# One token block's expert weights are added up in DRAM by indirect scatters

## The chip, the cores and the metric

The kernel runs on one core of one Trainium2 chip. The metric is the device time of one execution in microseconds; the time before is 1711.16 us, the median of three runs (1708.38 to 1712.05). Engine names are those of the profile: PE (TensorE), DVE (VectorE), ACT (ScalarE), POOL (GpSimd), SP (SyncE).

## The reference

One decoder block over 512 tokens of width 1024: two mixers with gates, then a product-key expert layer (PEER) over 16384 experts, then a norm. The change touches the expert layer alone:

```python
q = (xb @ w_q).reshape(TB, H, 2, PEER_HALF)             # 8 heads, two halves
s = jnp.einsum('thpc,phnc->thpn', q, sub_keys)           # 128 scores per half
s1, i1 = lax.top_k(s[:, :, 0], K); s2, i2 = lax.top_k(s[:, :, 1], K)      # K = 16
cand = (s1[..., :, None] + s2[..., None, :]).reshape(TB, H, K * K)
top_s, pos = lax.top_k(cand, K)                          # 16 experts per head
eidx = take(i1 * 128 + i2, pos)                          # 128 experts per token
g = softmax(top_s)
h = jnp.einsum('tkd,td->tk', u[eidx], xb)
out = jnp.einsum('tk,tkd->td', gelu(h) * g, v[eidx])
```

## The kernel before

The 512 tokens are four blocks (0 to 3) of 128. The kernel does the mixers first (projections, HGRN2 chains, gates, attention, up and output projections, to about 465 us). Then come three stages of the expert layer.

**Picks** (about 465 to 691 us). For each head h, `query` makes the two halves' queries for all four blocks, `scores` their scores, and `picks` (L670) finds with DVE's maximum and index instructions the 16 experts per token: e12 holds i1 and i2. Block 0's experts are written to eidx (L709), those of blocks 1 to 3 to iw12 (L711, ACT). Between the heads stand u chunks (`u_chunk`, L739): chunk j multiplies the 128 experts i*128+j with all tokens of blocks 1 to 3 (24 matmuls of 384 columns), Gelu on ACT, result to h_d in DRAM. Every chunk's weights are loaded by SP's queue and split into a high part (w_hi, ACT, L108) and a low part (w_lo, DVE, L110), double-buffered. 28 of the 128 chunks are done here (UH). After the last head `weigh` (L713) makes the softmax of all heads and blocks: gw0 for block 0, iw12's third plane for the others.

**One-hot stage** (about 692 to 949 us). Another 48 u chunks, and with each one group of 8 tokens of the weight matrix G[i, j, t] = sum of the weights with which token t picked expert i*128+j. `g_block` (L817) transposes a block's i1, i2 and weights; `g_group` (L834) builds one-hot rows on DVE (oz, ow, L845 and L847) and multiplies them on PE (16 matmuls of 128 columns, L855); ACT copies them out (L858), and each 32 tokens go to g_d by SP's queue (2 MB, L873). `work` (L861) lists 3 blocks x 16 groups = 48.

**V stage** (about 949 us to the end). The last 52 u chunks, and for each chunk j the product of G and Gelu(h) on DVE (`v_parts`, L903), split into aH and aL, times the experts' v rows: 18 matmuls of 512 columns, accumulated in PSUM over all 128 chunks. G comes back for four j at once (L901), Gelu(h) from h_d.

**Block 0** goes another way: POOL gathers for each of the 128 picks the 128 u rows (one per token) by an indirect DMA (`row`, L755, 512 KB), DVE multiplies with x (`u_row`, L762); later the same with v rows (`v_row`, L772). Four row buffers. In the picks no row is asked for (R0 = 0), in the one-hot stage one per chunk (R1 = 1, none for the last 8 chunks), in the V stage 2.9 and then 0.95.

The order of an engine's instructions is not the program's: a planning pass orders them by when their inputs are ready in its model of time, earlier calls first where several are ready. Every engine then runs its instructions strictly in that order, so a waiting one holds all behind it.

Of the kernel before, what the change touches and what calls it, by code (L numbers as in the profile page):

```python
# [10 lines left out]
F32 = mybir.dt.float32  # L11
# [3 lines left out]
I32 = mybir.dt.int32  # L15
# [3 lines left out]
OP = mybir.AluOpType  # L19
# [6 lines left out]
NB = 4  # L26
# [14 lines left out]
def trunk(ctx, tc, A, out, dbg=None):  # L41
# [173 lines left out]
    def proj_T(off, evac, t0=0):  # L215

        hi, lo = cut(weight(A["wT_%d" % off]), 8)
        ps = psum([P, S], "mm")
        for c in range(8):
            mm3(ps[:, :S - t0], (hi[:, c, :], lo[:, c, :]), (xnH[:, c, t0:], xnL[:, c, t0:]), c == 0, c == 7)  # L220
        evac(ps[:, :S - t0])
# [194 lines left out]
    def gate(m):  # L416
        def evg(ps):
            g = wk.tile([P, S], F32, name="t2k", bufs=4)
            dve.tensor_tensor(g, ps, rb, op=OP.mult)
            act.activation(g, g, AF.Sigmoid)  # L420
            act.dma_start(gate_d[m], g)
        proj_T(GA + m * P, evg)


# [136 lines left out]
    gffn = late.tile([P, D], F32, name="gffn")  # L561
    gfin = late.tile([P, D], F32, name="gfin")
    xf0 = late.tile([P, D], F32, name="xf0")
    eidx = late.tile([P, P], I32, name="eidx")
    gw0 = late.tile([P, P], F32, name="gw0")
    iw12 = late.tile([P, 3, 3, P], F32, name="iw12")
    NT = 3 * P
    xfs = ctx.enter_context(tc.tile_pool(name="xfs", reuse_waits="tile", side="right", bufs=1))
    xfH = xfs.tile([P, 8, S], F32R, name="xfH")
# [56 lines left out]
    rk = rks.enter_context(tc.tile_pool(name="rk", reuse_waits="tile", side="right", bufs=2))  # L626
    iota = rk.tile([P, 16], F32, name="iota", bufs=1)
    act.dma_start(iota, A["iota"][:, :16])
    tva = rk.tile([P, NB, 8, 16], F32, name="tva", bufs=1)
    io16k = rk.tile([P, 16, 16], F16, name="io16k", bufs=1)  # L630
    dve.tensor_copy(io16k, iota[:, :, None].to_broadcast([P, 16, 16]))
# [25 lines left out]
    def top16(trip):  # L657
# [9 lines left out]
        for val, pos, s in trip:  # L667
            dve.max_index(pos[:, 8:16], val[:, 8:16], s)

    def picks(h, sc2):  # L670


# [33 lines left out]
        e12 = rk.tile([P, 2, NB, 16], F32, name="e12")  # L706
        dve.tensor_tensor(e12.rearrange("p z b k -> p (z b) k"), oh[:, :, 0], oh[:, :, 1], op=OP.add)
        hs = slice(h * 16, (h + 1) * 16)
        dve.scalar_tensor_tensor(eidx[:, hs], e12[:, 0, 0], 128.0, e12[:, 1, 0], op0=OP.mult, op1=OP.add)  # L709
        for z in range(2):  # L710
            act.copy(iw12[:, :, z, hs], e12[:, z, 1:, :])  # L711

    def weigh():  # L713

        nm = rk.tile([P, NB, 8, 16], F32, name="nm", bufs=1)
        dve.tensor_tensor(nm, tva, tva[:, :, :, 0:1].to_broadcast([P, NB, 8, 16]), op=OP.subtract)
        act.activation(nm, nm, AF.Exp)
        ws = rk.tile([P, NB, 8], F32, name="ws")
        dve.tensor_reduce(ws, nm, axis=AX.X, op=OP.add)
        dve.reciprocal(ws, ws)  # L720
        for b in range(NB):
            o = gw0 if b == 0 else iw12[:, b - 1, 2, :]
            dve.tensor_tensor(o.rearrange("p (h k) -> p h k", h=8), nm[:, b], ws[:, b, :, None].to_broadcast([P, 8, 16]),
                              op=OP.mult)
# [7 lines left out]
    UPRE = sum(UH)  # L732
    R0, R1, R2, R3, NOROW = 0, 1, 2.9, 0.95, 8
    TG, QJ = 32, 4
    NG = NT // TG
    g_d = dram.tile([NG, P, P, TG], F32, name="g_d")
    h_d = dram.tile([LEAD, P, NT], F32, name="h_d")

# [16 lines left out]
    def row(tab, k):  # L755
        g = gp.tile([P, D], F32, name="row")
        pool.indirect_dma_start(out=g, out_offset=None, in_=A[tab],  # L757
                                in_offset=bass.IndirectOffsetOnAxis(ap=eidx[:, k:k + 1], axis=0))
        return g

    def u_row(k):
# [44 lines left out]
    with ExitStack() as st:  # L806
# [71 lines left out]
    accs = [[vp.tile([P, 512], F32, name="acc_%d_%d" % (b, n)) for n in range(2)] for b in range(3)]  # L878
    v3 = A["peer_v"].rearrange("(i j) d -> i j d", j=P)

    gq_t = [None]

    def v_parts(j, hgt):
        if j < LEAD and j % 2:

            raw = wst.tile([P, WN], F32, name="w_raw", bufs=3)[:, :D]
            vh = wst.tile([P, WN], F32R, name="w_hi")[:, :D]
            vl = wst.tile([P, WN], F32R, name="w_lo")[:, :D]
        else:
            raw = vt.tile([P, D], F32, name="v_raw")  # L890
            vh = vt.tile([P, D], F32R, name="v_hi")
            vl = vt.tile([P, D], F32R, name="v_lo")
        act.dma_start(raw, v3[:, j, :])
        act.copy(vh, raw)  # L894
        pace[0] = dve.tensor_tensor(vl, raw, vh.bitcast(F32), op=OP.subtract)  # L895
        if hgt is None:
            hgt = vs.tile([P, NT], F32, name="hgr")
            act.dma_start(hgt, h_d[j])
        if j % QJ == 0:
            gq_t[0] = vs.tile([P, NG, QJ, TG], F32, name="gj", bufs=2)  # L900
            act.dma_start(gq_t[0], g_d[:, :, j:j + QJ, :].rearrange("g i j t -> i g j t"))  # L901
        gj = vs.tile([P, NT], F32, name="aj")
        dve.scalar_tensor_tensor(gj.rearrange("p (g t) -> p g t", t=TG), gq_t[0][:, :, j % QJ, :], 1.0 / 16384,  # L903
                                 hgt.rearrange("p (g t) -> p g t", t=TG), op0=OP.mult, op1=OP.mult)
        aH = vs.tile([P, NT], F32R, name="aH")
        act.copy(aH, gj)  # L906
        aL = vs.tile([P, NT], F32R, name="aL")
        dve.tensor_tensor(aL, gj, aH.bitcast(F32), op=OP.subtract)  # L908
        return (aH, aL), (vh, vl)
# [147 lines left out]
```

## Time and profile before

| | |
|---|---|
| median of 3 runs | 1711.16 us |
| profiled execution | 1711.65 us, its span 1709.9 us |
| busy: PE, DVE, ACT, POOL | 1675.5, 1340.8, 729.3, 377.0 us |
| granted TensorE clock, mean | 0.996 |
| DMA | 414.90 MB, 243 GB/s over the span |
| DMA from 700 to 1600 us, by stretches of 100 us | 308 to 356 GB/s |
| indirect gathers on POOL | 256, of 1.39 us mean |

The span is the time from the first to the last instruction; the profiled execution's own time lies 1.75 us above it. Busy time counts an instruction from its start to its end; those of PE overlap.

### The profile page before, as it was taken

Reading aid. Unit: us, or ns where it says so; the run is one execution under the profiler, and the core shown is the slowest. Engines: PE = TensorE matmul, PEld = TensorE weight load, DVE = VectorE, ACT = ScalarE, POOL = GpSimd, SP = SyncE. Lnnn points to the kernel's source line nnn. Section 1 sums busy time; section 2 is a strip of 40 time slices with the busy share of each in tenths; the row PEclk is TensorE's granted clock in tenths of the full one; section 3 lists DMA queues with packets and bytes.
Section 4 is the critical chain, followed back from the end, with each engine's and each line's share of the span. In section 5 each row is a group of like instructions: output and inputs, shape, how many; then the busy total and the mean of one; then the engine's idle time right before and its main releaser. Section 6 shows DMA issues by size and latency. Waiting matters only on the chain.

```text
span 1709.9 us, 24687 instructions
## 1 busy us (share of the span) xinstructions
PE 1675.5 (98%) x9095; PEld 1465.9 (86%) x9097; DVE 1340.8 (78%) x2573; ACT 729.3 (43%) x1052; POOL 377.0 (22%) x284
## 2 busy tenths in 40 slices
PE   8999999999999999999999999999999999999997
PEld 6988887777798888999999999999999978888886
DVE  4776887547699999998988588878887888877785
ACT  4322226734443434566666433333333333333333
POOL 2000000000010000232322144444444442333320
PEclk9999999999999999999999999999999999999999
DMA  7321233127454334798988899999999999999983
GB/s 234 131 81 50 75 125 116 56 94 241 163 177 128 126 123 131 248 359 316 359 316 336 278 338 335 337 331 319 322 317 344 324 336 353 357 333 346 321 299 131
DMA packets 172472, 414.90 MB, mean 243 GB/s; under 512 B 14744, under 2 KB 85784, under 8 KB 170688
## 3 DMA queue, kind: packets, MB, share of 16 engines
q10 hardware_dynamic: 101072, 141.70, 24.4%
q1 hardware_dynamic: 34416, 137.40, 22.6%
q0 software_dynamic: 36864, 134.23, 22.4%
q8 instruction: 71, 1.16, 0.3%
q14 instruction: 49, 0.40, 0.1%
HBM read 366.86 MB, written 49.04 MB: 243 GB/s over the span
## 4 chain that ended last, share of the span: by engine, by line
PE 41%; issue 33%; DMA 11%; POOL 9%; DVE 5%; ACT 1%; POOLq 0%; SPq 0%; ACTq 0%; DVEq 0%
POOL row L757 8%; PE acc L79 6%; PE acc L77 6%; PE acc L78 6%; DMA row<-in_peer_u,eidx 5%; PE ps_mm L77 5%; PE ps_mm L79 5%; PE ps_mm L78 5%; DMA row<-in_peer_v,eidx 4%; PE ps_hg L379 2%; PE ps_hg L77 1%; PE ps_yb L460 1%; PE ps_hg L78 1%; PE ps_hg L79 1%; DMA v_raw<-in_peer_v 1%
## 5 line engine op out<-in xcount | busy, mean ns | idle before, releaser
L108 ACT CAST w_hi<-w_raw 128x1024 fp32r<-128x1024 f32 (+2 forms) x215 | 219.2, 1020 | 401.0 <-PE ps_u L78 125.4
L110 DVE TENSOR_TENSOR w_lo<-w_raw,w_hi 128x1024 fp32r<-128x1024 f32 (+2 forms) x215 | 254.9, 1185 | 84.4 <-ACT w_hi L108 72.1
L757 POOL DMA_INDIRECT row<-in_peer_u,eidx x128 | 178.5, 1394 | 553.6 <-DVE hh L762 503.6
L77 PE MATMUL ps_u<-xfH,w_hi 128*128 128x384 f32 x800 | 274.0, 343 | 1.4 <-ACT hg L744 1.4
L78 PE MATMUL ps_u<-xfL,w_hi 128*128 128x384 f32 x800 | 270.6, 338 | 0.0
L79 PE MATMUL ps_u<-xfH,w_lo 128*128 128x384 f32 x800 | 269.9, 337 | 0.0
L757 POOL DMA_INDIRECT row<-in_peer_v,eidx x128 | 178.6, 1395 | 275.5 <-DVE acc L772 253.3
L78 PE MATMUL acc<-v_lo,aH 128*128 128x512 f32 x540 | 211.2, 391 | 3.3 <-DVE v_lo L895 3.3
L77 PE MATMUL acc<-v_hi,aH 128*128 128x512 f32 x540 | 212.1, 393 | 1.4 <-ACT aH L906 1.1
L79 PE MATMUL acc<-v_hi,aL 128*128 128x512 f32 x540 | 212.1, 393 | 0.1
L906 ACT CAST aH<-aj 128x384 fp32r<-128x384 f32 x128 | 65.6, 513 | 308.7 <-DVE aj L903 138.1
L772 DVE SCALAR_TENSOR_TENSOR acc<-row,ah,acc 128x1024 f32<-128x1024 f32 x127 | 162.6, 1281 | 21.4 <-DMA row<-in_peer_v,eidx 20.7
L762 DVE CUSTOM_DVE_ANT_0 scr<-row,xf 128x1024 f32<-128x1024 f32 x128 | 156.3, 1221 | 20.1 <-DMA row<-in_peer_u,eidx 19.3
L77 PEld LDWEIGHTS ps_u<-xfH,w_hi 128*128 128x128 f32 x800 | 150.2, 188 | 3.5 <-ACT hg L744 1.7
L78 PEld LDWEIGHTS ps_u<-xfL,w_hi 128*128 128x128 f32 x800 | 150.5, 188 | 2.2
L79 PEld LDWEIGHTS ps_u<-xfH,w_lo 128*128 128x128 f32 x800 | 150.2, 188 | 0.0
L895 DVE TENSOR_TENSOR v_lo<-v_raw,v_hi 128x1024 fp32r<-128x1024 f32 x90 | 110.0, 1223 | 24.1 <-ACT v_hi L894 23.5
L78 PEld LDWEIGHTS acc<-v_lo,aH 128*128 128x128 f32 x540 | 101.7, 188 | 24.0 <-DVE v_lo L895 3.6
L79 PEld LDWEIGHTS acc<-v_hi,aL 128*128 128x128 f32 x540 | 101.8, 188 | 23.2 <-DVE aL L908 0.8
L77 PEld LDWEIGHTS acc<-v_hi,aH 128*128 128x128 f32 x540 | 101.7, 188 | 22.1 <-ACT aH L906 1.4
L894 ACT CAST v_hi<-v_raw 128x1024 fp32r<-128x1024 f32 x90 | 94.4, 1048 | 51.6 <-PE acc L79 19.9
L858 ACT COPY stg<-ps_g 128x512 f32<-128x512 f32 x96 | 99.6, 1158 | 3.3 <-PE ps_g L855 3.3
(313 smaller groups left out, 3367.4 us busy)
## 6 DMA issues: line engine op xcount, KB each, us to landing
w_raw<-in_uT SPq DMA_DIRECT2D x128, 512.0 KB
v_raw<-in_peer_v ACTq DMA_DIRECT2D x90, 512.0 KB
g_d<-stg SPq DMA_DIRECT2D x12, 2048.0 KB
gj<-g_d ACTq DMA_DIRECT2D x32, 768.0 KB
w_raw<-in_peer_v ACTq DMA_DIRECT2D x38, 512.0 KB
w_raw<-in_wT SPq DMA_DIRECT2D x31, 512.0 KB
h_d<-hg ACTq DMA_DIRECT2D x76, 192.0 KB
hgr<-h_d ACTq DMA_DIRECT2D x76, 192.0 KB
```

The lines of the kernel that those rows point to most:

```text
L77: pe.matmul(ps, lh, rh, start=first, stop=False, **kw)
L78: pe.matmul(ps, lh, rl, start=False, stop=False, **kw)
L79: pe.matmul(ps, ll, rh, start=False, stop=last, **kw)
L108: act.copy(hi[:, :n], raw[:, :n])
L110: pace[0] = dve.tensor_tensor(lo[:, :n], raw[:, :n], hi[:, :n].bitcast(F32), op=OP.subtract)
L757: pool.indirect_dma_start(out=g, out_offset=None, in_=A[tab], in_offset=bass.IndirectOffsetOnAxis(ap=eidx[:, k:k + 1], axis=0))
L762: dve.tensor_tensor_reduce(out=scr, in0=row("peer_u", k), in1=xf0, scale=1.0, scalar=0.0, op0=OP.mult, op1=OP.add, accum_out=hh[:, k:k + 1])
L772: dve.scalar_tensor_tensor(acc, row("peer_v", k), ah[:, k:k + 1], acc, op0=OP.mult, op1=OP.add)
L858: act.copy(stg[:, :, t4:t4 + 4].rearrange("p j t -> p t j"), ps)
L894: act.copy(vh, raw)
L895: pace[0] = dve.tensor_tensor(vl, raw, vh.bitcast(F32), op=OP.subtract)
L906: act.copy(aH, gj)
```

## The change

Block 3's part of G is no longer built by one-hot products. It is a table g3_d in DRAM of [expert, token], zeroed by four 2 MB DMAs issued from ACT's queue with the first four gates. In picks, each head now also takes the softmax of block 3's 16 best scores, computes the flat index expert*128 + token (gi), and POOL issues 16 indirect scatters per head (128 in all), each adding 128 weights of 4 bytes, one per token, to the table. The scatters of one head don't wait for one another; the first of a head waits until all of the head before have landed, since two heads may pick the same expert. The one-hot stage keeps blocks 1 and 2 (32 groups), weigh leaves block 3 out, and the V stage reads the table with a DMA of its own and multiplies block 3's columns in a second DVE instruction.

```diff
+    g3_d = dram.tile([P * P, P], F32, name="g3_d")
+    nil = consts.tile([P, 512], F32, name="nil")
+    pool.memset(nil, 0.0)
...
             act.dma_start(gate_d[m], g)
+            if m < 4:
+                act.dma_start(g3_d[m * 32 * P:(m + 1) * 32 * P, :].rearrange("(p r q) t -> p r (q t)", p=P, q=4),
+                              nil[:, None, :].to_broadcast([P, 8, 512]))
...
-    eidx = late.tile([P, P], I32, name="eidx")
+    eidx = late.tile([P, 2, P], I32, name="eidx")
+    pcol = late.tile([P, 1], F32, name="pcol")
...
+    scattered = []
+    def after(ins, others):
+        for o in others:
+            tc.add_manual_dep(ins.ins, o.ins.name, ...)
...
-        dve.scalar_tensor_tensor(eidx[:, hs], e12[:, 0, 0], 128.0, e12[:, 1, 0], op0=OP.mult, op1=OP.add)
+        dve.scalar_tensor_tensor(eidx[:, :, hs], e12[:, 0, 0:NB:3, :], 128.0, e12[:, 1, 0:NB:3, :], op0=OP.mult, op1=OP.add)
         for z in range(2):
-            act.copy(iw12[:, :, z, hs], e12[:, z, 1:, :])
+            act.copy(iw12[:, :, z, hs], e12[:, z, 1:3, :])
+        gi = rk.tile([P, 16], I32, name="gi", bufs=3)
+        act.activation(gi, eidx[:, 1, hs], AF.Identity, scale=128.0, bias=pcol)
+        mx = rk.tile([P, 1], F32, name="pmx")
+        dve.tensor_scalar(mx, tv[:, 3, 0:1], -1.0, None, op0=OP.mult)
+        wh = rk.tile([P, 16], F32, name="wh", bufs=3)
+        sm = rk.tile([P, 1], F32, name="psm")
+        act.activation(wh, tv[:, 3], AF.Exp, bias=mx, accum_out=sm)
+        dve.reciprocal(sm, sm)
+        act.activation(wh, wh, AF.Copy, scale=sm)
+        mine = []
+        for k in range(16):
+            ins = pool.indirect_dma_start(out=g3_d.rearrange("e (t one) -> (e t) one", one=1),
+                                          out_offset=bass.IndirectOffsetOnAxis(ap=gi[:, k:k + 1], axis=0),
+                                          in_=wh[:, k:k + 1], in_offset=None, compute_op=OP.add)
+            for o in mine:
+                tc.declare_no_dep(ins.ins, o.ins, reason="the 16 picks of a head are different experts")
+            if k == 0:
+                after(ins, scattered)
+            mine.append(ins)
+        scattered[:] = mine
...
-    NG = NT // TG
+    NG = 2 * P // TG
...
-        work = [(b, t0) for b in range(3) for t0 in range(0, P, TB)]
+        work = [(b, t0) for b in range(2) for t0 in range(0, P, TB)]
...
+            gq_t[1] = vs.tile([P, QJ, P], F32, name="gk", bufs=2)
+            after(act.dma_start(gq_t[1], g3_d.rearrange("(i j) t -> i j t", j=P)[:, j:j + QJ, :]), scattered)
...
-        dve.scalar_tensor_tensor(gj.rearrange("p (g t) -> p g t", t=TG), gq_t[0][:, :, j % QJ, :], 1.0 / 16384,
-                                 hgt.rearrange("p (g t) -> p g t", t=TG), op0=OP.mult, op1=OP.mult)
+        dve.scalar_tensor_tensor(gj[:, :2 * P].rearrange("p (g t) -> p g t", t=TG), gq_t[0][:, :, j % QJ, :], 1.0 / 16384,
+                                 hgt[:, :2 * P].rearrange("p (g t) -> p g t", t=TG), op0=OP.mult, op1=OP.mult)
+        dve.tensor_tensor(gj[:, 2 * P:], gq_t[1][:, j % QJ, :], hgt[:, 2 * P:], op=OP.mult)
```

## Rows read from the trace of the kernel before

**Rows 1.** The page's first part, busy us of each engine

```profile
PE 1675.5 (98%) x9095; PEld 1465.9 (86%) x9097; DVE 1340.8 (78%) x2573; ACT 729.3 (43%) x1052; POOL 377.0 (22%) x284
```

**Rows 2.** Stretches: us, then busy us per engine, clock, DMA share, GB/s

```profile
552.00:579.00 27.00, 26.10 (x139) 23.29 (x138) 25.50 (x115) 10.72 (x17) 0.00 (x0) 1.00 0.39 125
...
692.00:776.00 84.00, 83.18 (x644) 80.47 (x642) 73.20 (x81) 53.19 (x64) 25.43 (x16) 1.00 0.86 314
...
972.00:1380.00 408.00, 404.65 (x2033) 367.64 (x2031) 332.77 (x421) 142.53 (x195) 192.06 (x142) 1.00 0.93 328
...
195.00:240.00 45.00, 45.00 (x271) 39.52 (x270) 43.89 (x108) 11.00 (x16) 1.01 (x1) 1.00 0.27 88
```

**Rows 3.** Waits of PE in picks, one-hot stage, gates: us, times, longest

```profile
PE ps_mm L79 <- DVE w_lo L110: 3.5, 5, 0.8
...
PE ps_g L855 <- ACT stg L858: 2.4, 6, 0.5
...
PE ps_tr L410 <- DVE t2k L407: 1.2, 2, 0.7
```

**Rows 4.** ACT in time order: Gelu of u chunks (start us, us)

```profile
944.77 0.48 ACT L744 ACTIVATE hg<-ps_u 128x384 f32<-128x384 f32 x1
...
949.96 0.48 ACT L744 ACTIVATE hg<-ps_u 128x384 f32<-128x384 f32 x1
...
954.19 0.48 ACT L744 ACTIVATE hg<-ps_u 128x384 f32<-128x384 f32 x1
```

**Rows 5.** The same at the start of the one-hot's second block

```profile
781.23 0.49 ACT L744 ACTIVATE hg<-ps_u 128x384 f32<-128x384 f32 x1
...
785.74 0.48 ACT L744 ACTIVATE hg<-ps_u 128x384 f32<-128x384 f32 x1
...
793.09 0.48 ACT L744 ACTIVATE hg<-ps_u 128x384 f32<-128x384 f32 x1
```

**Rows 6.** One line, the attention's reciprocal: ns min/median/max

```profile
L463 DVE RECIPROCAL rs<-rs x4: 184/202/204, 295.1 to 368.6; 128x8 f32<-128x8 f32 x4
```

**Rows 7.** DVE in time order, the first w_lo of a head

```profile
579.24 1.23 DVE L110 TENSOR_TENSOR w_lo<-w_raw,w_hi 128x1024 fp32r<-128x1024 f32 x1 [1.17 <-ACT w_hi L108]
```

**Rows 8.** Table load and Exp: ACT and DVE in time order, one line

```profile
678.28 1.28 ACT L717 ACT_TABLE_LOAD   x1
...
679.42 0.67 DVE L716 TENSOR_TENSOR nm<-tva 128x512 f32<-128x512 f32 x1
...
680.01 0.19 DVE L692 TENSOR_SCALAR ab<-tp 128x64 uint32<-128x64 uint32 x1
...
L453 ACT ACTIVATE lg<-lg,lmx x32: 402/558/731, 262.9 to 367.7; 128x128 f32<-128x128 f32 x8, 128x256 f32<-128x256 f32 x8, 128x384 f32<-128x384 f32 x8, 128x512 f32<-128x512 f32 x8
```

**Rows 9.** POOL's gathers: chain of waits, time order, one tile

```profile
499.32 5.72 DMA row<-in_peer_u,eidx
...
499.32 1.47 POOL L757 DMA_INDIRECT row<-in_peer_u,eidx  x1 [37.90 <-ACT qT L644]
...
502.34 0.94 POOL L757 DMA_INDIRECT row<-in_peer_u,eidx  x1 [0.30 <-issue]
...
690.80 0.96 POOL L757 DMA_INDIRECT row<-in_peer_u,eidx  x1 [186.27 <-DVE hh L762]
...
710.02 1.68 POOL L757 DMA_INDIRECT row<-in_peer_u,eidx  x1 [4.01 <-DVE hh L762]
...
L757 POOL DMA_INDIRECT row<-in_peer_v,eidx x128: 939/1019/2619, 1195.7 to 1645.0; - x128
```

**Rows 10.** DVE and PE in time order, around row 4

```profile
710.81 1.22 DVE L110 TENSOR_TENSOR w_lo<-w_raw,w_hi 128x1024 fp32r<-128x1024 f32 x1
...
713.08 1.22 DVE L762 CUSTOM_DVE_ANT_0 scr<-row,xf 128x1024 f32<-128x1024 f32 x1
...
713.83 0.42 PE L77 MATMUL ps_u<-xfH,w_hi 128*128 128x384 f32 x1
```

**Rows 11.** One line, the V stage's product of G and h

```profile
L903 DVE SCALAR_TENSOR_TENSOR aj<-gj,hgr x76: 548/556/561, 1376.4 to 1685.5; 128x384 f32<-128x384 f32 x76
```

More of the change, by code (lines that the diff above doesn't have):

```diff
@@ L563, in trunk @@
     xf0 = late.tile([P, D], F32, name="xf0")
-    eidx = late.tile([P, P], I32, name="eidx")
+    eidx = late.tile([P, 2, P], I32, name="eidx")
+    pcol = late.tile([P, 1], F32, name="pcol")
     gw0 = late.tile([P, P], F32, name="gw0")
-    iw12 = late.tile([P, 3, 3, P], F32, name="iw12")
+    iw12 = late.tile([P, 2, 3, P], F32, name="iw12")
     NT = 3 * P
@@ L628, in trunk @@
     act.dma_start(iota, A["iota"][:, :16])
+    act.dma_start(pcol, bass.AP(tensor=A["iota"].tensor, offset=A["iota"].offset, ap=[[1, P], [1, 1]]))
     tva = rk.tile([P, NB, 8, 16], F32, name="tva", bufs=1)
@@ L668, in top16 @@
             dve.max_index(pos[:, 8:16], val[:, 8:16], s)
+    scattered = []
+    def after(ins, others):
+        for o in others:
+            tc.add_manual_dep(ins.ins, o.ins.name, mybir.DependencyInfo(mybir.DependencyClass.Sync, mybir.DependencyReason.DATA))
     def picks(h, sc2):
@@ L708, in picks @@
         hs = slice(h * 16, (h + 1) * 16)
-        dve.scalar_tensor_tensor(eidx[:, hs], e12[:, 0, 0], 128.0, e12[:, 1, 0], op0=OP.mult, op1=OP.add)
+        dve.scalar_tensor_tensor(eidx[:, :, hs], e12[:, 0, 0:NB:3, :], 128.0, e12[:, 1, 0:NB:3, :], op0=OP.mult, op1=OP.add)
         for z in range(2):
-            act.copy(iw12[:, :, z, hs], e12[:, z, 1:, :])
+            act.copy(iw12[:, :, z, hs], e12[:, z, 1:3, :])
[19 more added lines that the diff above has]
+        scattered[:] = mine
     def weigh():
-        nm = rk.tile([P, NB, 8, 16], F32, name="nm", bufs=1)
-        dve.tensor_tensor(nm, tva, tva[:, :, :, 0:1].to_broadcast([P, NB, 8, 16]), op=OP.subtract)
+        nm = rk.tile([P, 3, 8, 16], F32, name="nm", bufs=1)
+        dve.tensor_tensor(nm, tva[:, 0:3], tva[:, 0:3, :, 0:1].to_broadcast([P, 3, 8, 16]), op=OP.subtract)
         act.activation(nm, nm, AF.Exp)
-        ws = rk.tile([P, NB, 8], F32, name="ws")
+        ws = rk.tile([P, 3, 8], F32, name="ws")
         dve.tensor_reduce(ws, nm, axis=AX.X, op=OP.add)
         dve.reciprocal(ws, ws)
-        for b in range(NB):
+        for b in range(3):
             o = gw0 if b == 0 else iw12[:, b - 1, 2, :]
@@ L757, in row @@
         pool.indirect_dma_start(out=g, out_offset=None, in_=A[tab],
-                                in_offset=bass.IndirectOffsetOnAxis(ap=eidx[:, k:k + 1], axis=0))
+                                in_offset=bass.IndirectOffsetOnAxis(ap=eidx[:, 0, k:k + 1], axis=0))
         return g
@@ L879, in trunk @@
     v3 = A["peer_v"].rearrange("(i j) d -> i j d", j=P)
-    gq_t = [None]
+    gq_t = [None, None]
     def v_parts(j, hgt):
```

## The prediction

> **What bounds the kernel now.** I read the page's first part first: TensorE (PE) is busy for 98% of a span of 1709.9 us, no other engine for more than 78% [rows 1]. Then the stretches. The kernel's second half has three stages that the change touches: the picks (about 480 to 691 us, a period of 27 us for each head), the one-hot stage (692 to about 949) and the V stage after it. In the period shown for the picks PE is busy for 26.1 of 27 us and VectorE (DVE) for 25.5; in the first 84 us of the one-hot stage PE for 83.2, DVE for 73.2 and the DMA engines for 0.86; in the V stage PE for 404.7 of 408 [rows 2]. The clock is at its upper level, 1.00, in all of them. The view of waits says what PE lacks: in the picks 3.5 us for w_lo from DVE, in the one-hot stage 2.4 us for ScalarE (ACT) to free the one-hot PSUM tile [rows 3]. So a microsecond of matmul removed from the one-hot stage is a microsecond of time, as long as DVE, POOL or the DMAs don't become late; and in the picks DVE is within 1.5 us per head of being the bound. The page's chain of waits ends in row gathers and "issue", which is POOL waiting for its buffers; I don't build on it.
>
> **Removed.** Of the 48 one-hot groups 16 go, and one of three block starts. What a group costs PE is read from the evictions of the u chunks. With one group per chunk they follow each other after 5.19 us (944.77 to 949.96); the next, without a group, comes after 4.23 [rows 4]. A group costs 0.96 us: 16 x 0.96 = 15.4. At a block start the chunks came after 4.51 and 7.35 us (781.23, 785.74, 793.09), 11.86 against 2 x 5.19 = 10.38 [rows 5]: 1.5 us per block start. **Removed: 16.9 us.** What could be late next in that stage? DVE loses 32 instructions, ACT 32 copies, and the DMA queue four writes of 2 MB. A chunk has now 512 KB of weights, 192 KB out, 512 KB of one row and 2048/4 = 512 KB of G; with two groups in three chunks 341 KB of G. That is 1557 KB in 5.19 - 0.32 = 4.87 us, 327 GB/s, the 328 that the V stage moves with PE full [rows 2]. So PE stays the bound there and the 16.9 us stand.
>
> **Added to the picks, on DVE and ACT.** Per head DVE gets one negation of a column and one reciprocal, at most 0.20 us each by the reciprocal of 8 columns [rows 6]: 8 x 0.40 = 3.2 us. DVE has 1.17 us of idle time per head, before the head's first w_lo, which waits for ACT [rows 7]; so they cost between nothing and 3.2 us: I take 1. ACT gets Exp among Gelus: a table load of 1.28 us [rows 8], twice per head, for there and back; ACT is busy for 10.7 of 27 us [rows 2], so the time itself hides. But the reciprocal on DVE waits for the Exp, and behind it in DVE's order stand w_lo and the next head's maxima, for which PE waits. At worst a head loses a table load and the Exp (0.40 at the least) [rows 8], 1.68 us, 8 x 1.68 = 13 us. At best nothing: the order is not the program's. weigh()'s subtraction stands at 679.42 ahead of picks' shift at 680.01, and its table was loaded at 678.28, before its input was there [rows 8], so such instructions are slotted into gaps. I take 0.4 us per head, 3 us, being nearer to the rows where nothing was lost. **Sum in the picks: +4, bounds 0 to 16.**
>
> **Added on POOL.** A scatter has 128 indices like a row gather, so I price it by the gather: 0.94 us with 0.30 to the next where DVE runs maxima, 1.47 and 1.68 where DVE runs an instruction with two operands, 2.62 at most [rows 9]. Such DVE work (w_lo, the one-hot of the positions) is about 10 of a head's 27 us, so a scatter takes 1.24 + 0.38 x 0.74 = 1.52 us, 16 of them 24.3. A head's first scatter waits for the last head's to land; the first gather landed 5.72 us after its start, 4.25 after its descriptors [rows 9]: 24.3 + 4.25 = 28.5 against the period of 27. For 512 bytes instead of 512 KB I take the landing to be shorter and a backlog of nothing. POOL does nothing else in the picks; its first four gathers (499 to 505 us) become ready just ahead of head 0's scatters. The price is at the end: head 7's 16 scatters start when its picks are known, about 690, and the gather of row 4, at 690.80 today [rows 9], falls behind them. With 1.24 to 1.98 us each (16 x 1.24 = 20, 16 x 1.98 = 32) it starts at 710 to 722 and lands 5 to 6 us later, at 715 to 728. DVE wants row 4 at 713.08, and w_lo, queued behind it, has about 2 us to spare: it was done at 712.03 for a chunk that began at 713.83 [rows 10]. PE would lose 0 to 13 us, once; rows 5 to 7 then come 2 us apart and are wanted 5 us apart. The ordering may also put the u_row later, with no loss. **I take +5, bounds 0 to 13.**
>
> The Trainium skill speaks against this part. SBUF — State Buffer, "Who interferes with whom", says that a DVE instruction with two SBUF inputs contends with GpSimd, and an earlier section of that page ("A bandwidth-pool intuition that's wrong (but worth ruling out)") gives a DMA issued from GpSimd of some 620 ns that takes about 3100 ns beside a DVE copy. Rows 9 agree with the direction and show less, 0.94 to 1.68 us. By the page's ratio of five a scatter would be an estimated 4.7 us, and the sum would be the third rival's below. For the landing, DMA: Bandwidth & Descriptors, "Anatomy of one DMA — SWDGE (gpsimd) path", gives about 2.0 us fixed; by it a head's POOL work would be an estimated 26.3 us, just inside the period, by the row 28.5, just outside.
>
> **The rest.** Four zero fills of 2 MB go out beside the gates (200 to 240 us), where DMA is 0.27 busy [rows 2] and PE waits 1.2 us in all for 135 us [rows 3]. At the 328 GB/s of the V stage each takes 6.4 us, within one gate's time of 9: 0 to 3 us, I take 0.5. In the V stage a product of 0.56 us on DVE [rows 11] becomes two, at most 0.20 longer [rows 6], 26 us over the stage and beside PE's full time: nothing, DVE is at 333 of 408 [rows 2]. The reads of G keep their bytes in larger pieces: 0 to -3 us, I take 0.
>
> **Sum:** -16.9 + 4 + 5 + 0.5 = -7.4 us. The profiled execution took 1711.65 us (1709.9 of it the span), 0.5 above the median of 1711.16. 1711.65 - 7.4 = 1704.3: I predict **1704**. Within 0.2% (what a measurement of this kernel can't tell from no change) means 1707.8 to 1714.6.
>
> **Rivals.**
> - *Everything added hides* (0.17). For it: POOL is empty in the picks, instructions are slotted into gaps. Against: DVE's 1.5 us of slack per head. 1711.65 - 16.9 + 1 - 2 = 1694.
> - *Each head's DVE stands behind Exp and its table loads* (0.16). For it: DVE is 25.5 of 27 busy and the chain DVE, ACT, DVE, ACT is new. Against: weigh's chain in rows 8 passed without a stall. 1711.65 - 16.9 + 16 + 2 = 1713; no longer a gain from about 1.7 us per head.
> - *POOL can't keep up, and is slower than the picks* (0.16, slower). Place: POOL's queue between 498 us and row 4. It decides from the point where 16 scatters and the landing exceed 27 us, at about 1.5 us each. With 1.75 us it is 16 x 1.75 + 4.25 = 32.3, 5.3 us per head, 42 us over eight heads and late at row 4, for which DVE and then PE stand still: 1711.65 - 16.9 + 4 + 42 - 5 = 1736. With 2.92 (the longest gather, 2.62 + 0.30) it is 51 per head, 24 over, 192 us: about 1890, since the index buffers, three deep, then hold ACT as well. For it: 1.47 and 1.68 beside DVE's work. Against: 0.94 in the picks themselves.
> - *The change doesn't free the stage* (0.07): the groups go, but the one-hot stage runs into its DMAs. For it: 0.86 of their time. Against: four writes fewer, and 0.93 in the V stage with PE full. At the 314 GB/s of its first stretch [rows 2] 1557 KB take 5.08 us: 48 x 0.11 = 5 us saved, 1711.65 - 5 + 4 = 1711.
>
> **How the numbers follow.** My forecast (1697 to 1707.8) has 0.44. Faster by over 0.2%: 0.44 and 0.17 = 0.61. Same: 0.07, and two thirds of the second rival, 0.11: 0.18. Slower: the rest of it, 0.05, and 0.16: 0.21. The range reaches from 1691 (all hidden, 3 us from the V stage) to 1728, past the second rival and into the mild end of the third; the forecast's own is 1695 to 1711.
>
> **What would show it.** Right: 16 u chunks 4.2 us apart among 5.2 between 692 and 930; one-hot matmuls 512 instead of 768; PE's waits in the picks under 10 us; scatters of 1.0 to 1.7 us on POOL, 16 done before the next head's; DVE waiting once for row 4 at 710 to 720. Wrong: heads 29 us apart or more, DVE idle in the picks before a reciprocal, scatters above 1.7 us, head 7's scatters ending after 730, or PE waiting for w_raw in the gate stage or the one-hot stage.

## The result, and the profile after

The changed kernel takes **1787.09 us** (median of 6 runs, 1784.75 to 1791.85), the kernel before 1711.61 in the same session: a ratio of 1.0441 [1.0406, 1.0476]. The forecast was 1704 with a range of 1691 to 1728. It is the rival "POOL can't keep up" that happened, at more than its price of 1736, and with a second loss ahead of the picks that no rival had.

The page's first part of the changed kernel answers to [rows 1]: PE does less work and stands in a longer span, POOL has 232 us more.

```profile
PE 1665.8 (93%) x8836; PEld 1455.5 (82%) x8838; DVE 1318.7 (74%) x2683; ACT 720.9 (40%) x1063; POOL 609.2 (34%) x413
```

The stretches (us, then busy us of PE, PEld, DVE, ACT and POOL, clock, DMA share, GB/s) answer to [rows 2]. In the picks (515 to 690) POOL, which had been idle, is busy for 141 of 175 us; behind them is a stretch in which PE works for 30 of 100 us.

```profile
515.00:690.00 175.00, 170.48 (x891) 152.19 (x890) 167.18 (x764) 92.45 (x143) 141.48 (x78) 1.00 0.58 134
700.00:800.00 100.00, 30.00 (x179) 28.85 (x179) 22.91 (x34) 20.53 (x32) 80.46 (x48) 0.67 0.34 49
```

What ends that stretch is seen in the waits of PE and of DVE (us, times, longest) and in DVE's product with row 4, the first row gathered behind the picks, which in the kernel before began at 713.08 [rows 10]:

```profile
PE ps_g L895 <- DVE ow L887: 69.5, 1, 69.5
```

```profile
DVE scr L802 <- DMA row<-in_peer_u,eidx: 80.0, 11, 72.9
```

```profile
804.89 1.22 DVE L802 CUSTOM_DVE_ANT_0 scr<-row,xf 128x1024 f32<-128x1024 f32 x1 [72.87 <-DMA row<-in_peer_u,eidx]
```

DVE stands in one wait of 72.87 us for row 4. PE has used up what DVE had made and waits 69.5 us for the next one-hot tile, which is queued on DVE behind that row. The gather of row 4 is on POOL. Here is POOL in time order (start, us): scatters of head 0 and what follows them, and at the end the last scatter and the gather of row 4. The profile leaves out numbers in names: the g_d of a scatter is the table g3_d.

```profile
511.56 1.61 POOL L743 DMA_INDIRECT g_d<-wh,gi  x1 [0.30 <-issue]
513.47 1.56 POOL L743 DMA_INDIRECT g_d<-wh,gi  x1 [0.30 <-issue]
...
521.51 2.95 POOL L743 DMA_INDIRECT g_d<-wh,gi  x1 [0.30 <-issue]
...
544.17 1.56 POOL L743 DMA_INDIRECT g_d<-wh,gi  x1 [0.30 <-issue]
546.03 1.01 POOL L797 DMA_INDIRECT row<-in_peer_u,eidx  x1 [0.30 <-issue]
...
550.61 1.61 POOL L743 DMA_INDIRECT g_d<-wh,gi  x1 [0.30 <-issue]
...
798.44 1.56 POOL L743 DMA_INDIRECT g_d<-wh,gi  x1 [0.30 <-issue]
800.30 1.01 POOL L797 DMA_INDIRECT row<-in_peer_u,eidx  x1 [0.31 <-issue]
```

A scatter takes 1.56 us where [rows 9] had 0.94 to 0.96 for a gather, and up to 3 us. The 128 of them fill POOL from 511.56 to 800 almost without a gap, 37 us from one head's first scatter to the next ((770.47 - 511.56) / 7), while the picks of a head need 26.4. Their line over the whole run gives the mean, 1787 ns, and the tile's view gives min, median and max:

```profile
L743 POOL DMA_INDIRECT g_d<-wh,gi x128 | 228.7, 1787 | 55.5 <-issue 51.9
```

```profile
L743 POOL DMA_INDIRECT g_d<-wh,gi x128: 1555/1559/3015, 511.6 to 798.4; - x128
```

When do a head's picks become known? DVE writes eidx once per head; the first and the last of the kernel before, then the first two, the sixth and the last two of the changed kernel:

```profile
498.20 0.17 DVE L709 SCALAR_TENSOR_TENSOR eidx<-e 128x16 int32<-128x16 f32 x1
...
688.08 0.17 DVE L709 SCALAR_TENSOR_TENSOR eidx<-e 128x16 int32<-128x16 f32 x1
```

```profile
508.69 0.19 DVE L727 SCALAR_TENSOR_TENSOR eidx<-e 128x32 int32<-128x32 f32 x1
535.07 0.19 DVE L727 SCALAR_TENSOR_TENSOR eidx<-e 128x32 int32<-128x32 f32 x1
...
640.79 0.19 DVE L727 SCALAR_TENSOR_TENSOR eidx<-e 128x32 int32<-128x32 f32 x1
671.44 0.19 DVE L727 SCALAR_TENSOR_TENSOR eidx<-e 128x32 int32<-128x32 f32 x1
707.96 0.18 DVE L727 SCALAR_TENSOR_TENSOR eidx<-e 128x32 int32<-128x32 f32 x1
```

Heads 1 to 5 follow each other after 26.4 us, heads 6 and 7 after 30.7 and 36.5 (before mostly 26.87, the last 29.6; in no_scatter 26.4, the last 28.7). With the evictions (Gelu) of u chunk 28, the first of the one-hot stage, of chunk 76, the first behind it, and of chunk 127, the last, the whole span divides like this, for the two kernels and two of the experiments below (us; in brackets against before). Chunks 28 and 76 of the changed kernel, and under them of spread3:

```profile
718.33 0.48 ACT L784 ACTIVATE hg<-ps_u 128x384 f32<-128x384 f32 x1
...
1026.14 0.48 ACT L784 ACTIVATE hg<-ps_u 128x384 f32<-128x384 f32 x1
```

```profile
694.08 0.49 ACT L787 ACTIVATE hg<-ps_u 128x384 f32<-128x384 f32 x1
...
932.23 0.48 ACT L787 ACTIVATE hg<-ps_u 128x384 f32<-128x384 f32 x1
```

```
                              before   after            no_scatter       spread3
start to eidx of head 0       498.20   508.69 (+10.5)   509.26 (+11.1)   498.00 ( -0.2)
eidx of head 0 to of head 7   189.88   199.27 ( +9.4)   187.24 ( -2.6)   187.30 ( -2.6)
to chunk 28                     8.74    10.37 ( +1.6)     8.78 (  0.0)     8.78 (  0.0)
chunk 28 to chunk 76          253.14   307.81 (+54.7)   236.30 (-16.8)   238.15 (-15.0)
chunk 76 to chunk 127         422.24   417.49 ( -4.8)   423.20 ( +1.0)   417.40 ( -4.8)
to the end                    337.70   342.17 ( +4.5)   339.72 ( +2.0)   342.47 ( +4.8)
span                         1709.90  1785.80 (+75.9)  1704.50 ( -5.4)  1692.10 (-17.8)
```

Three things have to be explained: 10.5 us ahead of head 0, 12.0 us at heads 6 and 7 (9.4 + 2.6, against no_scatter), and a standstill of some 71 us in the one-hot stage (54.7 + 16.8).

### The profile page after: what moved, and what is told of

It reads as the page before. It is cut to its first block, busy times and chain, and to the rows that moved or that the text cites. A ratio compares the mean times of both kernels' runs of the same rounds, so it can differ in the third digit from the quotient of the medians.

```text
span 1785.8 us, 24463 instructions
## 1 busy us (share of the span) xinstructions
PE 1665.8 (93%) x8836; PEld 1455.5 (82%) x8838; DVE 1318.7 (74%) x2683; ACT 720.9 (40%) x1063; POOL 609.2 (34%) x413
## 4 chain that ended last, share of the span: by engine, by line
PE 52%; POOL 2%; DMA 2%; DVE 1%; issue 1%; ACT 0%; POOLq 0%; ACTq 0%; DVEq 0%
PE acc L79 9%; PE acc L77 9%; PE acc L78 9%; PE ps_u L77 7%; PE ps_u L78 7%; PE ps_u L79 7%; POOL g_d L743 2%; PE ps_g L895 2%; DMA v_raw<-in_peer_v 1%; DMA g_d<-stg 0%; DMA gj<-g_d 0%; DMA row<-in_peer_u,eidx 0%; DVE o_sum L967 0%; ACT stg L898 0%; DVE o_fin L969 0%
## 5 line engine op out<-in xcount | busy, mean ns | idle before, releaser
L797 POOL DMA_INDIRECT row<-in_peer_u,eidx x128 | 174.9, 1367 | 333.8 <-DVE hh L802 280.7
L797 POOL DMA_INDIRECT row<-in_peer_v,eidx x128 | 184.7, 1443 | 272.0 <-DVE acc L812 239.9
L743 POOL DMA_INDIRECT g_d<-wh,gi x128 | 228.7, 1787 | 55.5 <-issue 51.9
L71 POOL TENSOR_TENSOR rs_r<-rs_ms,half 128x1 f32<-128x1 f32 (+1 forms) x13 | 11.2, 864 | 370.5 <-DVE rs_ms L69 350.5
```

Of the source, the lines that this page charges most:

```text
L743: ins = pool.indirect_dma_start(out=g3_d.rearrange("e (t one) -> (e t) one", one=1), out_offset=bass.IndirectOffsetOnAxis(ap=gi[:, k:k + 1 ...
```

## The experiments

Theory A: the groups removed give what was predicted, and the scatters lose it because POOL needs longer for a head's 16 than the picks do, so that row 4 is late. Its rivals are named with each run. Ratios are to the kernel before, on the same chip.

**no_scatter: the scatters alone taken out.**

```diff
-        for k in range(16):
+        for k in range(0):
```

> Leaves out the 128 scatters alone (block 3's weights stay zero); gi, Exp, reciprocal, zero fills and the 32 one-hot groups stay. Theory A (POOL's queue: row 4's gather stands behind 128 scatters of 2.1 us, and the three wh buffers hold ACT for heads 6 and 7): the 72.9 us wait of DVE for row 4 and the 12.1 us of its two waits at the reciprocal go, head periods stay at 26.4 us to the last; 1787 - 70 - 11 - 3 (clock after the standstill) = 1703, faster than before but not by the full 16.9 us, since the 10.5 us lost before head 0 stay. Rival B (Exp and its table loads hold DVE): head periods of 28 us and over 1713. Rival C (the one-hot stage gives nothing back): about 1720.

1703.91 us, 0.9933 [0.9911, 0.9955]. The table above has its stages. ACT's Gelu of chunks 28, 76 and 77 here, and under it chunk 28 of the kernel before, whose chunk 76 is the 949.96 of [rows 4]:

```profile
705.28 0.49 ACT L784 ACTIVATE hg<-ps_u 128x384 f32<-128x384 f32 x1
...
941.58 0.48 ACT L784 ACTIVATE hg<-ps_u 128x384 f32<-128x384 f32 x1
945.80 0.49 ACT L784 ACTIVATE hg<-ps_u 128x384 f32<-128x384 f32 x1
```

```profile
696.82 0.48 ACT L744 ACTIVATE hg<-ps_u 128x384 f32<-128x384 f32 x1
```

236.30 against 253.14 us: the stage is shorter by 16.84 us, and a chunk without a group takes 4.22. Exp, its table loads and the reciprocal are all still in this kernel, and its heads follow after 26.4 us. So these cost nothing that shows, and the standstill and the late heads 6 and 7 come from the scatters. The loss ahead of head 0 is still there (509.26): it doesn't. The time is the 1703 that theory A gave.

**half and twelve: 8 and 12 of a head's 16 scatters.**

```diff
-        for k in range(16):
+        for k in range(0, 16, 2):     # half
+        for k in range(12):           # twelve
```

> Every second scatter is left out (64 of 128, half of block 3's picks are missing from G). Theory: 8 x 2.09 + 2.5 = 19.2 us for a head is less than the 26.4 us that a head takes, POOL keeps up, the last scatter ends before 720 us, DVE waits for row 4 under 10 us, time 1704 to 1708 us as without scatters. Rival (what the scatters move in the DMA queues stretches the picks and the rows behind them, whatever their number on POOL): half of the difference of 83 us stays, about 1745 us.

> 12 of a head's 16 scatters (a quarter of block 3's picks is missing from G). Theory (16 a head need 16 x 1.86 + 2.45 = 32.2 us at least, so the point from which POOL decides lies between 11 and 13 a head: 12 x 2.0 + 2.45 = 26.5 against 26.4): POOL falls behind by about 0 to 1 us a head, the last scatter ends at 725 to 735, DVE waits for row 4 for 5 to 20 us, time 1704 + 5 to 20 = 1709 to 1724 us, far from the middle between 8 scatters (1702) and 16 (1787). Rival (each scatter costs the same wherever POOL stands, 85 us / 64 = 1.3 us each above 64): 1702 + 32 x 1.3 = 1744 us.

half: 1701.92 us, 0.9944 [0.9923, 0.9965]; twelve: 1722.78, 1.0059 [1.0041, 1.0076]. POOL's line in half, and DVE's wait for row 4 in twelve:

```profile
L743 POOL DMA_INDIRECT g_d<-wh,gi x64 | 115.5, 1804 | 82.7 <-ACT gi L732 65.4 <-issue 16.8 <-DMA g_d<-wh,gi 0.6
```

```profile
738.03 1.23 DVE L802 CUSTOM_DVE_ANT_0 scr<-row,xf 128x1024 f32<-128x1024 f32 x1 [21.16 <-DMA row<-in_peer_u,eidx]
```

With 8 scatters POOL waits seven times for the next head's indices (gi), 65 us in all, so it keeps up; DVE's longest wait for a row is 1.4 us, and the time is 2 us under the expected window. A scatter itself is no cheaper there (1804 ns). With 12 POOL has run late by 21 us at row 4. The cost is not a price per scatter: the first 64 cost nothing, 32 more cost 21 us, the last 32 a further 64. It begins between 8 and 12 scatters a head, where theory A has a head's scatters and the landing pass 26.4 us, and both rivals' numbers (1745 and 1744) are missed.

**plain_write: the same scatters without the addition.**

```diff
-                                          in_=wh[:, k:k + 1], in_offset=None, compute_op=OP.add)
+                                          in_=wh[:, k:k + 1], in_offset=None)
```

> The same 128 scatters with the same waits, as plain writes instead of additions (where two heads of a token share an expert the last one's weight stands alone). Theory A1 (the addition makes the descriptors dearer): POOL takes 0.94 us at the least as for a row gather, 1.24 to 1.5 from one to the next, 16 with their landing 24 to 27 us per head, within the period of 26.4; row 4 is late by under 15 us and the time 1710 to 1722. Theory A2 (any scatter of 4-byte pieces costs 1.56 us): no change, 1787, and 1.86 us from one to the next.

1744.44 us, 1.0174 [1.0136, 1.0212]. The tile's view and POOL's line, to be read against the changed kernel's above:

```profile
L743 POOL DMA_INDIRECT g_d<-wh,gi x128: 965/970/2770, 513.8 to 754.4; - x128
```

```profile
L743 POOL DMA_INDIRECT g_d<-wh,gi x128 | 150.2, 1173 | 88.0 <-ACT gi L732 47.9 <-issue 40.1
```

A scatter without the addition takes 0.97 us at its least and median, with it 1.56: the addition costs 0.59 us of POOL's time for 128 indices. What comes on top of the median is much the same in both, 1173 - 970 = 203 ns and 1787 - 1559 = 228 ns on the mean; each of the 39 scatters of the changed kernel that took over 1.66 us ran beside a DVE instruction with two inputs. POOL here waits for ACT again (47.9 us), so it keeps up most of the time. The time was missed by more than 20 us all the same: the picks themselves became longer (eidx at 510.88, 547.50, ... 728.24 us, 31 a head). In some heads a cast of weights on ACT waited up to 14 us, while the DMA engines moved next to nothing (a share of 0.03 from 528 to 536 us). Here are that cast and PE's matmuls around it:

```profile
538.81 1.04 ACT L112 CAST w_hi<-w_raw 128x1024 fp32r<-128x1024 f32 x1 [14.05 <-remote]
```

```profile
532.39 0.40 PE L78 MATMUL ps_mm<-xfL,w_hi 128*128 128x512 f32 x1 [0.93 <-issue]
532.62 0.39 PE L79 MATMUL ps_mm<-xfH,w_lo 128*128 128x512 f32 x1
539.91 0.79 PE L77 MATMUL ps_mm<-xfH,w_hi 128*128 128x512 f32 x1 [6.90 <-issue]
```

Its load was not late: it had been issued at 512.43 and had landed at 515.36. The cast waits for PE to give a buffer of w_hi free. PE signals that at 538.79, though its last matmul on record ends at 533.01, and from 529 us on its matmuls stand apart with no wait that the profile names ("issue"). In the two longest of these waits (14.05 and 11.97 us) the cast begins 3.8 and 1.7 us after the last scatter of its head has ended (534.99 and 659.55 us), which points at the scatters; what held PE was not found. It stays open, and only the price of the instruction is taken from this run.

**deep: 8 buffers for gi and wh instead of 3.**

```diff
-        gi = rk.tile([P, 16], I32, name="gi", bufs=3)
+        gi = rk.tile([P, 16], I32, name="gi", bufs=8)
...
-        wh = rk.tile([P, 16], F32, name="wh", bufs=3)
+        wh = rk.tile([P, 16], F32, name="wh", bufs=8)
```

> gi and wh have 8 buffers instead of 3. Theory (the chain of scatters on POOL sets when row 4 can be gathered): heads 6 and 7 are back at 26.4 us, eidx of head 7 at 697 us, but the last scatter still ends at 798 to 800, so that DVE's wait for row 4 grows by the same 11 us to about 84, and the time stays at 1787 +- 3. Rival (the late heads 6 and 7 are a loss of their own): 1776 us.

1786.54 us, 1.0446 [1.0405, 1.0487]. In the changed kernel ACT's Exp waits for a buffer that a scatter still reads, and DVE's reciprocal behind it for ACT; with 8 buffers that is gone (eidx of head 7 at 693.44), and the wait for row 4 is longer by 14.7 us:

```profile
665.33 1.28 ACT L737 ACT_TABLE_LOAD   x1 [9.41 <-DMA g_d<-wh,gi]
...
701.93 0.16 DVE L738 RECIPROCAL psm<-psm 128x1 f32<-128x1 f32 x1 [8.15 <-ACT wh L737]
```

```profile
DVE scr L802 <- DMA row<-in_peer_u,eidx: 102.1, 17, 87.6
```

The late heads were no loss of their own: POOL's chain ends at 799 to 800 us with either.

**rows_late: no row wanted in the first 18 chunks of the one-hot stage, more per chunk later.**

```diff
-    R0, R1, R2, R3, NOROW = 0, 1, 2.9, 0.95, 8
+    R0, R1, R2, R3, NOROW = 0, 1.25, 3.15, 0.95, 8
...
-            some_rows(R1 if j < LEAD - NOROW else 0)
+            some_rows(R1 if UPRE + 18 <= j < LEAD - NOROW else 0)
```

> The changed kernel with block 0's rows asked for from the 19th chunk of the one-hot stage on (R1 = 1.25 for 22 chunks, R2 = 3.15 instead of 2.9), so that DVE wants row 4 near 800 us, when POOL is through with its scatters; all scatters stay. Theory A: DVE's and PE's wait of 70 us shrinks to under 10, the time to 1787 - 65 - 3 + 0 to 8 (rows crowded into fewer chunks) = 1719 to 1727; head 7 still waits for wh. Rival E (slow scatters hurt by other ways, on the DMA queues or on DVE's port): over 1745.

1735.91 us, 1.0139 [1.0107, 1.0171]. The standstill is gone (DVE's longest wait for a row is 4.0 us) and 51 of its 71 us with it, though the scatters end at 811 us here. So it was row 4, not G, for which all stood. It is 9 us more than the upper end expected: chunk 76 comes 13.4 us later than in no_scatter (954.97), mostly by head 7, which still waits for wh (its eidx 9.2 us later), and the V stage up to chunk 127, into which the rows now crowd, takes 434.0 instead of 423.2 us.

**late_zero, start_clean, fill16: the zeros.** In the changed kernel the four fills of 2 MB don't run beside the gates: they are issued at 21.9 to 63.3 us, and 40 to 60 us has a DMA share of 0.99 where before had 0.54. The Sigmoid of the first gate comes at 208.82 instead of 199.66 us: 9.2 of the 10.5 us are lost ahead of the gates. late_zero binds each fill behind its gate's Sigmoid; start_clean makes the tile of zeros on ACT in the first gate instead of by a memset at the start; fill16 does that too and writes 16 pieces of 0.5 MB.

```diff
+            sig = act.activation(g, g, AF.Sigmoid)            # late_zero
...
+              with tc.issue_after(sig.ins):
...
-    pool.memset(nil, 0.0)                                     # start_clean, fill16
+            if m == 0:
+                act.activation(nil, g, AF.Copy, scale=0.0)
...
-            if m < 4:                                         # fill16
-                act.dma_start(g3_d[m * 32 * P:(m + 1) * 32 * P, :]...
-                              nil[:, None, :].to_broadcast([P, 8, 512]))
+            act.dma_start(g3_d[m * 8 * P:(m + 1) * 8 * P, :]...
+                          nil[:, None, :].to_broadcast([P, 2, 512]))
```

> The changed kernel with each zero fill tied behind the Sigmoid of its gate on ACT (issued at 200 to 236 us instead of 22 to 63). Theory A: the 10.5 us by which head 0's picks come later (498.2 to 508.7) are the 8 MB of zero fills that meet the first weight loads; head 0's eidx returns to 498 to 500 and the time falls by 8 to 10 us to 1778, all the rest shifted as it is. Rival D (the planner's other order in the first 470 us): head 0 stays at 507 to 509 and the time at 1787.

> The tile of zeros is made on ACT in the first gate instead of by the memset on POOL at the start; nothing else differs from the changed kernel. Theory (the zero fills that run at 22 to 63 us, and what their place does to the order of the first loads, cost the whole 10.5 us before head 0): the fills stand at 200 to 240 us, eidx of head 0 is back at 498 to 500 us, DMA share at 40 to 60 us back near 0.54, time 1787 - 10 = 1777 us. Rival (only the 4 us that late_zero gave back belong to the fills, the rest to something else in the stages before the picks): eidx of head 0 at 504, 1782 us. The wait for row 4 stays 68 to 73 us by both.

> The changed kernel with its 8 MB of zeros written as 16 transfers of 0.5 MB, one behind each of the 16 gates (200 to 325 us), instead of four of 2 MB; the zeros are made on ACT in the first gate. Theory (what is lost before head 0 is the DMA time of the fills where they stand together: DMA share 0.77 at 200 to 240 us in start_clean, against 0.30 before, with DVE 6 us later at 253 than at 222): eidx of head 0 at 498 to 501, against 505.6 in start_clean and 508.7 in the changed kernel; time 1787 - 9 = 1778 us, the wait for row 4 unchanged at about 70. Rival (the 6 us are the 3 added operations in the gates and another order, not the transfers): 505, 1783 us.

late_zero: 1782.39 us, 1.0403 [1.037, 1.0436], eidx of head 0 at 504.66. start_clean: 1783.57, 1.0409 [1.0373, 1.0445], at 505.56. fill16: 1776.59, 1.0372 [1.0343, 1.0401], at 500.71 (before 498.20). All wait about 70 us for row 4. Of the three, late_zero and start_clean miss what their theories gave (1778 and 1777), fill16 meets it (1778). The other kernels with the fills where the change put them (no_scatter, half, twelve, plain_write, deep, rows_late) have 506.28 to 510.88, so that late_zero and start_clean are hardly outside of their spread, and fill16 is. The stretch of the gates, 200 to 240 us, in before, start_clean and fill16, and in late_zero from 205 us, where its gates begin (PE's busy time is the first figure behind the length):

```profile
200.00:240.00 40.00, 40.00 (x244) 35.21 (x243) 39.10 (x95) 9.64 (x15) 1.01 (x1) 1.00 0.30 99
```

```profile
200.00:240.00 40.00, 37.02 (x206) 30.77 (x206) 39.55 (x98) 8.16 (x13) 0.00 (x0) 1.00 0.77 278
```

```profile
200.00:240.00 40.00, 40.00 (x248) 35.36 (x247) 39.42 (x95) 11.13 (x16) 0.00 (x0) 1.00 0.82 293
```

```profile
205.00:245.00 40.00, 40.00 (x243) 35.13 (x242) 39.56 (x95) 9.24 (x15) 0.00 (x0) 1.00 0.81 296
```

start_clean moved the loss and did not remove it: from the first gate's Sigmoid to the fifth's it takes 41.4 us (200.47 to 241.85), where before, fill16 and late_zero take 35.7. The next weights are cast at 219.21 instead of 207.79. ACT in start_clean, and under it in fill16:

```profile
218.68 0.63 ACT L423 ACTIVATE t2k<-t2k 128x512 f32<-128x512 f32 x1 [8.49 <-DVE t2k L422]
219.21 1.03 ACT L111 CAST w_hi<-w_raw 128x1024 fp32r<-128x1024 f32 x1
```

```profile
209.37 1.04 ACT L111 CAST w_hi<-w_raw 128x1024 fp32r<-128x1024 f32 x1 [6.45 <-PE ps_mm L78]
210.33 0.63 ACT L423 ACTIVATE t2k<-t2k 128x512 f32<-128x512 f32 x1
```

The late cast doesn't wait for its weights: they were issued at 183.11 and had landed at 186.65, before the first fill went out at 202.19. In ACT's order it stands behind the third gate's Sigmoid, which waits 8.49 us for DVE; in fill16, as in before, it stands ahead of the second's. And it isn't the share or the size of the transfers, as I had expected: fill16's 16 pieces also stand together, at 203 to 236 us, with a DMA share of 0.82, late_zero's four pieces of 2 MB with 0.81, and PE loses nothing in either. late_zero had lost its 5 us before the gates, with no fill issued yet (its first Sigmoid at 204.97 instead of 199.66). So what the traces show beside the gates is the order of ACT's instructions, which the planning pass sets; why it set this one was not tested. Of the 10.5 us in the changed kernel, fill16 gets 8 back with the fills moved; how much of that is DMA time at 22 to 63 us and how much another order stays open.

**spread, spread2, spread3: what theory A asks for.** The whole function, with gi and wh kept for all heads, fewer scatters in the picks, and the others one to a chunk of the one-hot stage behind that chunk's row on POOL. There a chunk of 4.2 to 5.2 us has POOL busy for little more than a row. The zeros are made as in start_clean, from spread2 on as in fill16.

```diff
-        for k in range(16):
-            ins = pool.indirect_dma_start(...
+        todo.extend(range(h * 16, h * 16 + 16))
+        scatter(11)                      # spread; spread2, spread3: 11 if h < 7 else 3
...
             some_rows(R1 if j < LEAD - NOROW else 0)
+            with tc.issue_after(last_row[0].ins):
+                scatter(1)               # spread3: (1 + (j % 5 == 0)) if j < LEAD - NOROW else 0
```

> The whole function. The tile of zeros made on ACT in the first gate; gi and wh kept for all heads; 11 scatters a head during the picks (88), the other 40 one to a chunk of the one-hot stage, behind that chunk's row gather on POOL. Theory (POOL is short of time only during the picks: 11 x 2.09 + 2.5 = 25.5 us is under 26.4, and in the one-hot stage a chunk of 4.2 to 5.2 us holds a row of 0.94 to 1.7 and a scatter of about 2): 1711.65 - 16.84 (groups) - 2.6 (heads) + 3 (V stage) + 0 to 5 (rows that come late, crowding) = 1695 to 1700 us, faster than the kernel before. Rival (scatters and row gathers share the queue, each row's landing is put off by the scatter ahead of it, or the picks stretch as soon as the queue is nearly full): 1710 us or more, with waits of DVE for rows all along the one-hot stage.

> The whole function: as spread, but heads 0 to 6 emit 11 scatters each during the picks and head 7 only 3, the other 48 one to a chunk of the one-hot stage, and the fills stand in 16 parts behind the 16 gates. Theory (all that spread lost against the kernel without scatters were two waits for rows, 12.5 and 7.8 us, behind the scatters of heads 6 and 7, and 6 to 7 us before head 0): 1714 - 16 - 6 = 1692 us, 1689 to 1698, faster than the kernel before; the 28th to the 76th Gelu take 237 to 240 us. Rival (the rows behind head 6's scatters are late whatever head 7 does, or the scatters of the last chunks, up to 945 us, hold the first gather of block 3 by the V stage): 1703 to 1712 us.

> The whole function: as spread2, but the 48 scatters that are left for the one-hot stage stand in the 40 chunks that have a row gather, one in each and two in every fifth, so that none are left to crowd ahead of a row in the last 8 chunks. Theory (the 8.2 us that spread2 lost at the 68th to the 70th chunk are the wait of 8.87 us for the row behind nine scatters in a stretch, 865.91 to 885.57 us): that wait is under 3 us and the time 1703 - 8 = 1695 us, 1692 to 1699. Rival (two scatters between two rows hold the row as well, 8 times about 1 to 2 us): 1700 to 1706.

spread: 1714.36 us, 1.0022 [1.0002, 1.0042]. spread2: 1702.95, 0.9942 [0.992, 0.9964]. spread3: **1695.92**, 0.9915 [0.9895, 0.9936]. DVE's longest waits for rows in the one-hot stage of each:

```profile
728.43 1.24 DVE L809 CUSTOM_DVE_ANT_0 scr<-row,xf 128x1024 f32<-128x1024 f32 x1 [12.52 <-DMA row<-in_peer_u,eidx]
757.08 1.22 DVE L809 CUSTOM_DVE_ANT_0 scr<-row,xf 128x1024 f32<-128x1024 f32 x1 [7.77 <-DMA row<-in_peer_u,eidx]
```

```profile
890.45 1.22 DVE L807 CUSTOM_DVE_ANT_0 scr<-row,xf 128x1024 f32<-128x1024 f32 x1 [8.87 <-DMA row<-in_peer_u,eidx]
```

```profile
735.72 1.23 DVE L807 CUSTOM_DVE_ANT_0 scr<-row,xf 128x1024 f32<-128x1024 f32 x1 [5.39 <-DMA row<-in_peer_u,eidx]
```

spread had the rival's time, but not its picture of waits all along the stage: there are two, behind the scatters of head 7, which end at 724 us just where row 4 is due, and its chunks are later by 16 us from there on than they would be without. spread2 takes head 7's scatters out, and loses 8 us at one place that I had overlooked: the last 8 chunks have no new row, so that their scatters, bound behind the last row, stood nine together (865.91 to 885.57 us) ahead of the rows of the V stage. spread3 puts them elsewhere and gives the 8 us back. It is faster than the changed kernel, and than the kernel before by 0.85%. Its stages in the table are near the forecast's: -15.0 us in the one-hot stage (forecast -16.9), -2.6 in the picks (forecast +4).

## Why the prediction was wrong

The step that failed is this one: "A scatter has 128 indices like a row gather, so I price it by the gather". That gave 0.94 + 0.30 and 0.28 for DVE's interference, 1.52 us. Measured are 1.56 + 0.30 = 1.86 at least and 1.79 + 0.30 = 2.09 on the mean. The interference was right, 0.23 against 0.28. The base was wrong by 0.62, of which plain_write shows 0.59 to be the addition. A row that moves 512 KB priced an instruction's indices well and said nothing of its operation, and the trace of before had no row with the addition. For 16 scatters the 0.57 are 9.1 us a head, and the step's result, 24.3 us against a period of 27, turned into 33.4 against 26.4.

The rival's own formula with the measured price, 16 x 2.09 + 4.25 = 37.7, is 10.8 over a period of 26.9 and 86 over eight heads: 1711.65 - 16.9 + 4 + 86 - 5 = 1780. So its mechanism and its point of decision, some 1.5 us a scatter, were right; half and twelve show that point from both sides. I gave it 0.16 and let the range end in its mild part, although the term that decides it was the one with no row of its own. That the sum comes so near has some luck in it: its landing of 4.25 us is too long by 0.3 to 2.1, and it knows nothing of the 10.5 us ahead of the picks.

Term by term:
- *Removed, -16.9:* measured -16.84 in no_scatter. That PE stays the bound of the shorter stage was right too: it works for 234.7 of the 236.3 us.
- *Picks on DVE and ACT, +4:* -2.6. Heads follow after 26.4 us with Exp, table loads and reciprocal in place, so the rival in which DVE stands behind Exp is false. DVE waits there only where ACT waits for a scatter's buffer. A head became 0.45 us shorter because PE idles less: before it works for 170.02 of 175 us of the picks, in no_scatter for 172.92, which by their periods is 26.1 us a head in both, and 0.76 and 0.31 idle.

```profile
515.00:690.00 175.00, 170.02 (x900) 153.29 (x898) 166.70 (x727) 71.67 (x107) 0.00 (x0) 1.00 0.39 128
```

```profile
515.00:690.00 175.00, 172.92 (x911) 155.92 (x911) 171.07 (x781) 94.99 (x146) 0.55 (x1) 1.00 0.42 137
```

- *POOL, +5, bounds 0 to 13:* 81.3 between the spans of no_scatter and the changed kernel, with 12.0 at heads 6 and 7 and 71.5 in the one-hot stage, at row 4. The place was named (row 4 behind head 7's scatters); the size is the price above. A head's landing was shorter than the row's 4.25 us, as supposed: the gaps between two heads' scatters on POOL are 2.4 to 4.2 us, with the 0.30 in them.
- *Zero fills, +0.5, bounds 0 to 3:* +10.5. "Four zero fills go out beside the gates" failed: nothing in the code holds a fill until its gate, since its source is ready from the start. Where they do go out there, in late_zero and fill16, the gates take as long as before, so the price itself was not wrong. Ahead of head 0 these kernels still lose 6.5 and 2.5 us, and start_clean, whose gates take 5.7 us longer, 7.4.
- *V stage, 0:* +3.0 in no_scatter, within what its runs scatter.

The Trainium skill, which spoke against the POOL part, was right in direction alone. By SBUF — State Buffer, "Who interferes with whom", a DVE instruction with two SBUF inputs contends with a GpSimd instruction that reads SBUF; the prediction leaves that condition out. The trace agrees in direction: the last 16 scatters, with DVE at a standstill, run at 1.56 to 1.58 us each, while those beside DVE's work reach 3.02. The ratio of five, from the earlier section of the same page of the Trainium skill, is not seen: the mean is 1.15 times the least. Nor does that ratio give the third rival's sum, as the prediction says: with an estimated 4.7 us the rival's formula has 16 x 5.0 + 4.25 = 84 us a head, far past the 1890. DMA: Bandwidth & Descriptors of the Trainium skill, "Anatomy of one DMA — SWDGE (gpsimd) path", gives a fixed 2.0 us. The gaps of 2.4 us between the late heads, less the 0.30, agree.

## What to carry to other kernels

Price an instruction by a row with the same operation, not by one with the same shape; where there is none, take the whole distance to the point from which it decides as open, and give the case beyond that point the chance that goes with it. An engine that "does nothing else" in a stage still has a first customer behind the new work: compare the work per period with the period, and if it is over, the backlog is paid at that customer, all at once. Work that has no deadline can be spread over the stages in which its engine has room (here 80 scatters in the picks and 48 in the one-hot stage), but look for the chunk in which the thing it is tied to doesn't occur.

## What was not expected of the hardware

- An indirect scatter of 128 elements of 4 bytes occupies POOL for 0.97 us, the same with an addition in DRAM for 1.56.
- 8 MB of zeros beside the gates took no time from PE at a DMA share of 0.81 to 0.82, in four transfers (late_zero) or in 16 (fill16).
- In the stretch of the standstill, 700 to 800 us, with PE busy for 30 of 100 us, the granted clock is 0.67 on the mean, between its two levels (1.2 and 2.4 GHz are 0.5 and 1.0), where before it was 1.00. The one-hot stage lost 71.5 us in all against 69.5 of PE's wait, which leaves some 2 us for the clock and all else.
- Plain 4-byte scatters came with heads in which PE gave a weight buffer free 5.8 us after its last matmul on record had ended (533.01 to 538.79), with idle DMA engines; the cause is open.
